# Second attention of an encoder layer: the loads of the values wait for the unit's last exponential, and four transposes and two products get new places

## The chip, the cores and the metric

The kernel runs on one core of one Trainium2 chip. The metric is the device time of one launch in microseconds (us), the median of several runs of the same kernel.

## What is computed

One layer of an encoder, for two groups of 2048 tokens with 1024 features. The change touches the second of its two attentions only:

```
h = rms_norm(x, norm_w);  q_b, k_b, v_b, g_b = parts of h @ w_in
q_b, k_b = rms_norm(q_b), rms_norm(k_b)             # per head, 8 heads of 64
s   = q_b . k_b / 8 + bias(row, col)                # tokens lie on a grid of 32 x 64;
s   = -inf outside the window of 8 rows x 16 cols   # bias is a learned table
o_b = softmax(s) @ v_b * silu(g_b)
x   = x + concat(o_a, o_b) @ w_out;  x = x + (p @ w_ple) * sigmoid(x @ w_ple_gate)
```

## The kernel before

The work runs in three stages: the first attention with its projections (to about 807 us), the second attention (to about 1840 us), and the output products. Every fp32 operand of a large product is split in a high and a low part, and three of the four partial products are summed.

The second attention is done in 64 units (`unit_b(f)`, f from 32 to 95). A unit is 128 queries (8 grid rows x 16 columns) of 4 heads, against 288, 360, 384 or 480 keys, by its place on the grid. Its actions, and the names of their tiles, are:

- `sc(0..3)`, one per head: scores on PE into `scb`; DVE adds the bias and takes the row maximum (`softmax`, L277) into `s`.
- `exp` (`exps`, L301): ACT takes four exponentials. Behind the second, third and fourth of them ACT issues DMAs (L310) that copy the heads' rows `s` into `tn`, a tile of another number type; the last two copies are issued behind the last exponential. In the same action `load_values` issues the loads of the values (L903), three or four DMAs of up to 256 KB on SP's queue, from `v_d` in DRAM into `vw`.
- `fin` of the unit before, `prep` for the next one.
- `pt(0..3)`: PE turns one head's copied rows (`ptb<-rowwise,tn`, L262); ACT and DVE write high and low parts into `p_t`.
- `po(0..3)`: PE multiplies `vw` and `p_t` into `pob`. The first two of these products run at the end of the unit, the last two in the next unit's start.

PE's order is written out and pinned: between the actions a generator hands out the projections of later tiles (24 products `pqk` and 24 `pvg` per unit, 128x512 each), and `PLAN_B` says at which fraction of the unit's budget (10,320 units of cost, 215 for one projection product) each action is put. Its rows are (fraction, 1 for this unit or 0 for the one before, action, index). On the other engines and in SP's queue the compiler layer orders the instructions by the times that it assumes; each queue is then worked through in order.

The bias table of the next unit (L888, `bias`) is loaded with a wait already: `last_ex[0]` is the last exponential issued so far, and `after(load, last_ex[0])` makes a DMA wait for it. The last six units (f of 90 and more) make no copies: their transposes read `s` itself.

SP's queue carries besides: the inputs of later tiles (`stx`, L361), the stores of values (`v_d<-vb`, L846) and results (`ob_d`), and, once in the stage, the new weights for the second half of the heads (`wa<-sp_1wa`, `wb<-sp_1wb`, L197, sixteen loads of 512 KB, issued around 1193 to 1231 us).

Of the kernel before, what the change touches and what calls it, by code (L numbers as in the profile page):

```python
# [11 lines left out]
F32 = mybir.dt.float32  # L12
# [7 lines left out]
NT = SEQ // 128  # L20
# [9 lines left out]
def window(b, cb):  # L30
    c0, nc_ = COL_WIN[cb]
    r0, nr = ROW_WIN[b]
    rows = 5 if nr == 15 and nc_ == 24 else 4
    return r0, nr, c0, nc_, rows


def chunks(nr, rows):

    first = list(range(0, nr - rows, rows)) + [nr - rows]
    return [(k, min(rows, z - k)) for k, z in zip(first, first[1:] + [nr])]  # L40


def row_type(b):
    return (0, 1, 1, 2)[b]


def col_type(cb):
    return (0, 1, 1, 2)[cb]


def query_rows(b, cb, j):

    r0, nr, _, _, rows = window(b, cb)
    k, n = chunks(nr, rows)[j]
    see = [r for r in range(8) if r0 + k - 7 <= min(max(8 * b + r - 4, 0), 24) <= r0 + k + n - 1]
    return (see[0], max(see[-1] + 1, 4)) if see[0] == 0 else (min(see[0], 4), see[-1] + 1)


def bias_offsets():
# [30 lines left out]
AHEAD = 5  # L90
# [8 lines left out]
PLAN_B = (  # L99
    (0.00, 1, "sc", 0), (0.03, 1, "sc", 1), (0.07, 1, "sc", 2), (0.09, 0, "po", 2), (0.11, 1, "sc", 3), (0.16, 0, "po", 3),  # L100
    (0.16, 1, "exp", 0), (0.24, 0, "fin", 0), (0.35, 1, "prep", 0),
    (0.68, 1, "pt", 0), (0.75, 1, "pt", 1), (0.82, 1, "pt", 2), (0.86, 1, "po", 0), (0.90, 1, "pt", 3), (0.95, 1, "po", 1),
)


def emit(ctx, tc, io):
    nc = tc.nc
# [4 lines left out]
    def ptile(shape, tag, name):  # L112
        tag = PSM.get(tag, tag)
        return pp.tile(shape, F32, tag=tag, name=name, bufs=PSB[tag])
# [142 lines left out]
    def mm(out, lhsT, rhs, start, stop):  # L257
        pinned(nc.tensor.matmul(out, lhsT, rhs, start=start, stop=stop))  # L258

    def tr(out, in_, eye=ident):  # L260
        if in_.dtype == F32R:
            pinned(nc.tensor.transpose(out.bitcast(F32R), in_, eye))  # L262
        else:
            pinned(nc.tensor.transpose(out, in_, eye.bitcast(F32)))  # L264
# [8 lines left out]
    def softmax(i, ps, n, bias, sm, s=None):  # L273

        if s is None:
            s = main.tile([128, 512], F32, tag="s", name="s", bufs=SB)[:, :n]
        nc.vector.tensor_tensor_reduce(out=s, in0=ps[:, :n], in1=bias, scale=1.0, scalar=-3.0e38,  # L277
                                       op0=ALU.add, op1=ALU.max, accum_out=sm["mx"][:, i:i + 1])
        sm["s"].append(s)

    def sm_tiles():
        return {"s": [], **{k: ap.tile([128, 4], F32, tag=k, name=k, bufs=3) for k in ("mx", "nm", "den", "rd")}}

    last_ex = []

    def after(ins, other):

        tc.add_manual_dep(ins.ins, other.name, mybir.DependencyInfo(mybir.DependencyClass.Sync, mybir.DependencyReason.DATA),
                          reason="behind the copies")
# [111 lines left out]
    def big(shape, dt, name):  # L401
        return ap.tile(shape, dt, tag="big", name=name, bufs=3)
# [81 lines left out]
    for i in range(2):  # L484
# [5 lines left out]
    v_d = {(half, s, cb): dram.tile([32, COL_WIN[cb][1], 4, 2, HD], F32, tag=f"v_d{half}{s}{cb}", name=f"v_d{half}{s}{cb}")  # L490
           for half in range(2) for s in range(2) for cb in range(4)}
# [382 lines left out]
    def unit_b(f):  # L874
        half, st = divmod(f - 2 * NT, 2 * NT)
        s, j = divmod(st, NT)
        b, cb = divmod(j, 4)
        _, gs = held[f]
        r0, nr, c0, ncol, rows = window(b, cb)
        kc, ch = rows * ncol, chunks(nr, rows)  # L880
        nch, kn = len(ch), [ncol * n for _, n in ch]
        n = nr * ncol
        if cb != 2:
            off, _ = BIAS_OFF[(row_type(b), col_type(cb))]
            if not bt:
                bt.append(big([128, 2, 4, 512], F32, "bias"))
            bt.append(bt[0][:, len(bt) % 2])
            load = nc.sync.dma_start(bt[-1][:, :, :n],  # L888
                                     io["bias"][half][:, off:off + 4 * n].rearrange("p (h n) -> p h n", h=4))
            if last_ex:  # L890
                after(load, last_ex[0])
        bias = bt[-1]
        vw = []

        def load_values():

            spare = f >= 6 * NT - 6 and f % 2 == 0
            if spare:
                four = ap.tile([128, 4, 4, 2 * HD], F32R, tag="raw", name="vw4", bufs=1)
            for j in range(nch):  # L900
                v = four[:, j] if spare else \
                    ap.tile([128, 4, 2 * HD], F32R, tag=("vp", "vr_")[j % 2], name="vw", bufs=3 - j % 2)
                nc.sync.dma_start(v[:kn[j]].bitcast(F32).rearrange("p h d -> p (h d)"),  # L903
                                  v_d[half, s, cb][r0 + ch[j][0]:r0 + sum(ch[j])]
                                  .rearrange("r c h a d -> (r c) (h a d)"))
                vw.append(v)

        sees = [query_rows(b, cb, j) for j in range(nch)]
        order = sorted(range(nch), key=lambda j: sees[j][1] - sees[j][0])
        at = [16 * sum(z - a for a, z in sees[:j]) for j in range(nch + 1)]  # L910
        sm, p_ts, got = sm_tiles(), [], {}

        def sc(h):
            ps = ptile([128, 512], "sc", "scb")
            for j, q in enumerate(qs[f]):
                mm(ps[:, :n].rearrange("p (r c) -> p r c", c=ncol), q[h % 2][:, 128 * (h // 2):128 * (h // 2) + 128],
                   ks_b[h % 2][:, r0:r0 + nr, h // 2, c0:c0 + ncol], j == 0, j == 1)
            softmax(h, ps, n, bias[:, h, :n], sm)
            if h == 3:
                if not tn:  # L920
                    tn.append(ap.tile([128, 4, 480], F32R, tag="ev", name="tn", bufs=1))
                got["ex"] = exps(sm, hr_b[:, st:st + 1], gs, turned=tn[0] if f < 6 * NT - AHEAD - 1 else None)
                next(got["ex"])

        def pt(x):
            h = (0, 2, 1, 3)[x]
            pt = ptile([128, 512], "pt", "ptb")
            for j in order:

                c = at[j] - 16 * sees[j][0]  # L930
                k0 = ncol * ch[j][0]
                tr(pt[:kc, c:c + 128], sm["s"][h][:, k0:k0 + kc], rowwise)
            p_t = main.tile([128, 2, 512], F32R, tag="p_t", name="p_t", bufs=3)
            hi, lo, pf = p_t[:kc, 0, :at[-1]], p_t[:kc, 1, :at[-1]], pt[:kc, :at[-1]]
            nc.scalar.copy(hi, pf)  # L935
            nc.vector.tensor_tensor(out=lo, in0=pf, in1=hi.bitcast(F32), op=ALU.subtract)  # L936
            p_ts.append(p_t)

        def po(x):
            h = (0, 2, 1, 3)[x]  # L940
            e, i = h % 2, h // 2
            if i == 0:
                got["po"] = ptile([128, 2, 256], "ms", "pob")
            if x == 0:
                got["ot"] = ap.tile([128, 2, 2, 128], F32, tag="ot", name="otb", bufs=2)
            po, ot = got["po"], got["ot"]
            for j in order[::-1]:
                a, z = sees[j]
                mm(po[:, i, :].rearrange("p (a q) -> p a q", a=2)[:, :, 16 * a:16 * z], vw[j][:kn[j], h, :],
                   p_ts[x][:kn[j], :, at[j]:at[j + 1]], j == order[-1], j == order[0])  # L950
            if i == 1:
                a, z = 64 * e, 64 - 64 * e
                pq = po.rearrange("p i (a q) -> p i a q", a=2)
                nc.scalar.copy(ot[a:a + 64], pq[z:z + 64])  # L954
                nc.vector.tensor_tensor(out=ot[a:a + 64], in0=pq[a:a + 64], in1=ot[a:a + 64], op=ALU.add)

        def fin(_):
            pgt = ptile([128, 2, 128], "sc", "pgtb")
            for i in range(2):
                tr(pgt[:, i, :], sm["g2"][:, 128 * i:128 * i + 128], rowwise)  # L960
            o_t = ap.tile([128, 2, 128], F32, tag="o_t", name="o_tb", bufs=2)
            nc.gpsimd.tensor_tensor(out=o_t, in0=got["ot"][:, :, 0], in1=got["ot"][:, :, 1], op=ALU.add)
            nc.vector.tensor_tensor(out=o_t, in0=pgt, in1=o_t, op=ALU.mult)
            nc.sync.dma_start(ob_d[s][b, :, 2 * half:2 * half + 2, cb, :], o_t)
        return {"sc": sc, "pt": pt, "po": po, "fin": fin, "prep": lambda _: nxt(f),
                "exp": lambda _: (next(got["ex"]), load_values())}


# [500 lines left out]
```

## Time and profile before

| | us |
|---|---|
| median of 3 runs | 2489.0 (2488.42 to 2490.54) |
| the profiled execution, its own time | 2492.04 |
| its span, first to last instruction | 2490.3 |
| PE busy in the span | 2447.5 (98%) |
| PE weight loads | 2060.5 (83%) |
| DVE, ACT, POOL busy | 1705.6, 1412.8, 853.1 |

The profiled execution is 3.0 us above the median of the runs. PE is busy nearly all the time, so what there is to win or lose from the order of work is in the 43 us in which PE stands still, and in what would be added to them. In a row of the view of waits stand the waiting instruction, what released it, the total of the waits in us, their number, and the longest.

### The profile page before, as it was taken

Reading aid. Unit: us, or ns where it says so; the run is one execution under the profiler, and the core shown is the slowest. Engines: PE = TensorE matmul, PEld = TensorE weight load, DVE = VectorE, ACT = ScalarE, POOL = GpSimd, SP = SyncE. Lnnn points to the kernel's source line nnn. Section 1 sums busy time; section 2 is a strip of 40 time slices with the busy share of each in tenths; the row PEclk is TensorE's granted clock in tenths of the full one; section 3 lists DMA queues with packets and bytes.
Section 4 is the critical chain, followed back from the end, with each engine's and each line's share of the span. In section 5 each row is a group of like instructions: output and inputs, shape, how many; then the busy total and the mean of one; then the engine's idle time right before and its main releaser. Section 6 shows DMA issues by size and latency. Waiting matters only on the chain. (4 is left out here: it accounts for less than half of the span.)

```text
span 2490.3 us, 40934 instructions
## 1 busy us (share of the span) xinstructions
PE 2447.5 (98%) x13062; PEld 2060.5 (83%) x13062; DVE 1705.6 (68%) x4215; ACT 1412.8 (57%) x3408; POOL 853.1 (34%) x1363
## 2 busy tenths in 40 slices
PE   8999999999999999999899999999999999999999
PEld 7888888888888888888778888887777888888887
DVE  6777777777765666666566666776537655686776
ACT  6777777777764665665456566665663222354443
POOL 4555555555543544554344444443110000000000
PEclk9999999999999999999999999999999999999999
DMA  6422233322354677767967787777977455756765
GB/s 208 134 97 94 88 103 98 97 94 87 102 178 153 203 252 234 232 210 228 336 217 228 225 266 255 244 247 266 316 232 272 163 171 175 265 176 217 242 227 170
DMA packets 279288, 485.55 MB, mean 195 GB/s; under 512 B 31617, under 2 KB 120097, under 8 KB 274849
## 3 DMA queue, kind: packets, MB, share of 16 engines
q1 hardware_dynamic: 245376, 437.84, 54.1%
q10 hardware_dynamic: 33696, 45.09, 5.3%
q8 instruction: 104, 1.70, 0.3%
q14 instruction: 112, 0.91, 0.1%
HBM read 307.72 MB, written 134.23 MB: 177 GB/s over the span
## 5 line engine op out<-in xcount | busy, mean ns | idle before, releaser
L258 PE MATMUL pqk<-wa,xr 128*128 128x512 f32 x1536 | 452.5, 411 | 0.0
L258 PE MATMUL pvg<-wb,xr 128*128 128x512 f32 x1536 | 450.6, 406 | 0.0
L301 ACT ACTIVATE s<-s,nm 128x320 f32<-128x320 f32 (+6 forms) x512 | 293.5, 575 | 131.1 <-DVE nm L298 119.1
L258 PEld LDWEIGHTS pvg<-wb,xr 128*128 128x128 f32 x1536 | 272.5, 190 | 34.1
L1254 ACT CAST opd<-raw 128x512 fp32r<-128x512 f32 x224 | 131.7, 619 | 270.6 <-PE acca L1272 117.9
L258 PEld LDWEIGHTS pqk<-wa,xr 128*128 128x128 f32 x1536 | 257.1, 188 | 29.7
L379 POOL TENSOR_TENSOR xr<-stx,xr 128x512 fp32r<-128x512 f32 x186 | 238.6, 1296 | 107.5 <-ACT xr L378 77.7
L1255 DVE TENSOR_TENSOR opd<-raw,opd 128x512 fp32r<-128x512 f32 x224 | 146.6, 686 | 145.6 <-ACT opd L1254 145.6
L258 PE MATMUL pg<-wb,xr 128*128 128x512 f32 x768 | 233.0, 409 | 1.0 <-DVE vv L536 1.0
L258 PE MATMUL pq<-wa,xr 128*128 128x512 f32 x768 | 219.3, 400 | 0.0
L954 ACT COPY otb<-pob 64x512 f32<-64x512 f32 x128 | 74.5, 582 | 213.3 <-PE pob L258 213.1
L936 DVE TENSOR_TENSOR p_t<-ptb,p_t 128x368 fp32r<-128x368 f32 (+5 forms) x256 | 121.6, 487 | 91.3 <-ACT p_t L935 88.7
L1272 PE MATMUL accc<-opd,wb 128*128 128x512 f32 x768 | 177.0, 389 | 0.5 <-DVE r L1317 0.5
L1272 PE MATMUL acca<-opd,wa 128*128 128x512 f32 (+1 forms) x780 | 176.2, 386 | 0.8 <-ACT r L1350 0.5
L1272 PE MATMUL acca<-opd,s 128*128 128x512 f32 x768 | 175.4, 389 | 0.0
L1272 PEld LDWEIGHTS acca<-opd,wa 128*128 128x128 f32 x780 | 144.9, 188 | 30.9 <-ACT ev L1050 0.8
L1272 PEld LDWEIGHTS accc<-opd,wb 128*128 128x128 f32 x768 | 144.1, 188 | 30.8 <-DVE r L1317 1.0
L1272 PEld LDWEIGHTS acca<-opd,s 128*128 128x128 f32 x768 | 144.2, 188 | 29.9
L143 POOL TENSOR_TENSOR yb<-vrb,power 128x8 f32<-128x8 f32 x64 | 106.5, 1664 | 175.7 <-DVE vrb L813 158.0
L935 ACT CAST p_t<-ptb 128x368 fp32r<-128x368 f32 (+5 forms) x256 | 107.5, 427 | 86.5 <-PE ptb L262 74.6
L258 PEld LDWEIGHTS pob<-p_t,vw 128*128 128x128 f32 (+2 forms) x832 | 132.6, 189 | 24.6 <-DVE p_t L936 4.4
L258 PEld LDWEIGHTS pq<-wa,xr 128*128 128x128 f32 x768 | 135.1, 189 | 17.3
(174 smaller groups left out, 5188.1 us busy)
## 6 DMA issues: line engine op xcount, KB each, us to landing
stx<-x_b SPq DMA_DIRECT2D x128, 256.0 KB
vw<-v_d SPq DMA_DIRECT2D x96, 256.0 KB
stx<-x_a SPq DMA_DIRECT2D x64, 256.0 KB
stn<-x_n SPq DMA_DIRECT2D x64, 256.0 KB
v_d<-vb SPq DMA_DIRECT2D x64, 256.0 KB
ple_d<-ev SPq DMA_DIRECT2D x64, 256.0 KB
xres<-x_r SPq DMA_DIRECT2D x64, 256.0 KB
x_d<-r SPq DMA_DIRECT2D x64, 256.0 KB
```

The source lines that it names most:

```text
L143: nc.gpsimd.tensor_tensor(out=y, in0=v, in1=power.broadcast_to([128, n]), op=ALU.pow)
L258: pinned(nc.tensor.matmul(out, lhsT, rhs, start=start, stop=stop))
L301: ex = nc.scalar.activation(ss[i], ss[i], AF.Exp, bias=nm[:, i:i + 1], accum_out=den[:, i:i + 1])
L379: low.tensor_tensor(out=lo, in0=raw, in1=hi.bitcast(F32), op=ALU.subtract)
L935: nc.scalar.copy(hi, pf)
L936: nc.vector.tensor_tensor(out=lo, in0=pf, in1=hi.bitcast(F32), op=ALU.subtract)
L954: nc.scalar.copy(ot[a:a + 64], pq[z:z + 64])
L1254: P(nc.scalar.copy(hi, v))
L1255: P(nc.vector.tensor_tensor(out=lo, in0=v, in1=hi.bitcast(F32), op=ALU.subtract))
L1272: pinned(nc.tensor.matmul(ps[:, cols], w[k][:, a, c:c + 128], o[:, b, cols], start=i in (0, 1, 4) and k == 0 and j == 0, stop=k == 3 and j ...
```

## The change

Two things change. In `PLAN_B` the four transposes `pt` go from 0.68, 0.75, 0.82, 0.90 of the unit to 0.60, 0.68, 0.76, 0.91, and the products `po(0)` and `po(1)` from 0.86 and 0.95 to 0.88 and 0.96. In `load_values` each load of values waits for `last_ex[0]`, which is there the last exponential of the unit that the values are for, in the 58 units that make copies.

```diff
 PLAN_B = (
     (0.00, 1, "sc", 0), (0.03, 1, "sc", 1), (0.07, 1, "sc", 2), (0.09, 0, "po", 2), (0.11, 1, "sc", 3), (0.16, 0, "po", 3),
     (0.16, 1, "exp", 0), (0.24, 0, "fin", 0), (0.35, 1, "prep", 0),
-    (0.68, 1, "pt", 0), (0.75, 1, "pt", 1), (0.82, 1, "pt", 2), (0.86, 1, "po", 0), (0.90, 1, "pt", 3), (0.95, 1, "po", 1),
+    (0.60, 1, "pt", 0), (0.68, 1, "pt", 1), (0.76, 1, "pt", 2), (0.88, 1, "po", 0), (0.91, 1, "pt", 3), (0.96, 1, "po", 1),
 )
...
-                nc.sync.dma_start(v[:kn[j]].bitcast(F32).rearrange("p h d -> p (h d)"),
-                                  v_d[half, s, cb][r0 + ch[j][0]:r0 + sum(ch[j])]
-                                  .rearrange("r c h a d -> (r c) (h a d)"))
+                load = nc.sync.dma_start(v[:kn[j]].bitcast(F32).rearrange("p h d -> p (h d)"),
+                                         v_d[half, s, cb][r0 + ch[j][0]:r0 + sum(ch[j])]
+                                         .rearrange("r c h a d -> (r c) (h a d)"))
+                if f < 6 * NT - AHEAD - 1:
+                    after(load, last_ex[0])
                 vw.append(v)
```

On PE, in the second half of one unit of 384 keys (the rows from the first product of the next tile's `pqk` to the unit's first `po`), before:

```order
L258 MATMUL pqk<-wa_9501,xr 128x512 x3
L258 MATMUL pqk<-wa_9503,xr 128x512 x3
L258 MATMUL pqk<-wa_9505,xr 128x512 x3
L262 MATMUL ptb<-rowwise,tn 128x128 x3
L258 MATMUL pqk<-wa_9507,xr 128x512 x3
L262 MATMUL ptb<-rowwise,tn 128x128 x3
L258 MATMUL pqk<-wa_9509,xr 128x512 x3
L258 MATMUL pqk<-wa_9511,xr 128x512
L262 MATMUL ptb<-rowwise,tn 128x128 x3
L258 MATMUL pqk<-wa_9511,xr 128x512 x2
L258 MATMUL pob<-p_t,vw 128x256
```

and the same place after the change:

```order
L258 MATMUL pqk<-wa_9501,xr 128x512 x3
L258 MATMUL pqk<-wa_9503,xr 128x512 x2
L262 MATMUL ptb<-rowwise,tn 128x128 x3
L258 MATMUL pqk<-wa_9503,xr 128x512
L258 MATMUL pqk<-wa_9505,xr 128x512 x3
L262 MATMUL ptb<-rowwise,tn 128x128 x3
L258 MATMUL pqk<-wa_9507,xr 128x512 x3
L258 MATMUL pqk<-wa_9509,xr 128x512
L262 MATMUL ptb<-rowwise,tn 128x128 x3
L258 MATMUL pqk<-wa_9509,xr 128x512 x2
L258 MATMUL pqk<-wa_9511,xr 128x512 x3
```

The first transposes stand behind 5 projection products instead of 9, the second behind 9 instead of 12, the third behind 13 instead of 16. The first `po` stands behind 19 instead of 18, the last transposes behind 20 as before, the second `po` behind 23 instead of 22.

In SP's queue, from a unit's `ob_d` store of results to the loads of values behind it, in a quiet part of the stage, before:

```order
L964 DMA ob_d_92<-o_tb 128x2x128
L888 DMA bias<-bias 128x4x288
L846 DMA v_d_312<-vb 8x8x512
L846 DMA v_d_313<-vb 16x8x512
L846 DMA v_d_314<-vb 8x8x512
L646 DMA sums_243<-raw 128x2048
L361 DMA stx<-x_b 128x512 x2
L903 DMA vw<-v_d_309 128x512
L903 DMA vw<-v_d_308 96x512
L903 DMA vw<-v_d_309 128x512
```

and another such stretch after:

```order
L966 DMA ob_d_91<-o_tb 128x2x128
L903 DMA vw<-v_d_312 120x512 x3
L888 DMA bias<-bias 128x4x480
L846 DMA v_d_313<-vb 8x8x512
L846 DMA v_d_314<-vb 16x8x512
L846 DMA v_d_315<-vb 8x8x512
L646 DMA sums_243<-raw 128x2048
L361 DMA stx<-x_b 128x512 x2
```

Before, the loads stand ahead of the unit's `ob_d` store, and some of them already fetch values of the next unit; after, all loads of a unit stand behind that store, and the bias table of the next unit stands behind the loads.

Where the new weights come in, SP's queue before (from the second load of `wa` to the inputs `stx`; the numbers at the names count the tensors):

```order
L197 DMA wa_15564<-sp_1wa_211 128x1024
L903 DMA vw<-v_d_308 120x512
L197 DMA wa_15566<-sp_1wa_212 128x1024
L964 DMA ob_d_92<-o_tb 128x2x128
L197 DMA wa_15568<-sp_1wa_213 128x1024
L197 DMA wa_15570<-sp_1wa_214 128x1024
L197 DMA wa_15572<-sp_1wa_215 128x1024
L197 DMA wa_15574<-sp_1wa_216 128x1024
L197 DMA wa_15576<-sp_1wa_217 128x1024
L888 DMA bias<-bias 128x4x480
L846 DMA v_d_309<-vb 8x8x512
```

and after:

```order
L966 DMA ob_d_92<-o_tb 128x2x128
L197 DMA wa_15566<-sp_1wa_212 128x1024
L903 DMA vw<-v_d_308 120x512 x3
L197 DMA wa_15568<-sp_1wa_213 128x1024
L197 DMA wa_15570<-sp_1wa_214 128x1024
L197 DMA wa_15572<-sp_1wa_215 128x1024
L197 DMA wa_15574<-sp_1wa_216 128x1024
L197 DMA wa_15576<-sp_1wa_217 128x1024
L846 DMA v_d_309<-vb 8x8x512
L846 DMA v_d_310<-vb 16x8x512
L846 DMA v_d_311<-vb 8x8x512
L888 DMA bias<-bias 128x4x480
```

Here the third load of `wa` goes behind the `ob_d` store, all three loads of values stand between the third and the fourth `wa`, and the bias table of the next unit goes behind the three stores of values.

## The prediction

> **What bounds the kernel now.** I read the waits of PE first, because PE is busy 98% of the span and a microsecond counts only where PE loses it. The five longest:
>
> ```profile
> PE ptb L262 <- DMA tn<-s: 15.8, 18, 3.1
> PE pk L258 <- issue: 7.3, 1, 7.3
> PE scb L258 <- DVE mx L277: 3.6, 2, 2.5
> PE pple L258 <- DVE qg L850: 1.8, 1, 1.8
> PE pob L258 <- DVE p_t L936: 1.7, 4, 0.8
> ```
>
> The transposes wait 15.8 us in 18 places for the copies `tn`; that is the one wait that the change aims at. A product that waits for the values' landing does not occur among them. Next I cut the second attention into stretches, by busy time, with PE and the DMA share in each (columns: stretch, its length, PE, PEld, DVE, ACT, POOL busy, clock, DMA share, GB/s):
>
> ```profile
> 806.70:1174.60 367.90, 364.59 (x2017) 304.73 (x2016) 244.72 (x620) 221.75 (x528) 181.43 (x205) 1.00 0.72 228
> 1174.60:1285.50 110.90, 100.37 (x536) 80.96 (x535) 64.03 (x162) 58.03 (x139) 45.26 (x53) 0.98 0.88 289
> 1285.50:1683.10 397.60, 395.72 (x2190) 330.56 (x2189) 273.43 (x691) 253.82 (x592) 177.25 (x208) 1.00 0.75 240
> 1683.10:1757.40 74.30, 67.84 (x361) 55.41 (x360) 45.22 (x111) 40.15 (x95) 21.60 (x28) 0.98 0.84 283
> ```
>
> PE stands still for 3.3, 10.5, 1.9 and 6.5 us. The second stretch is the six units in which the new weights are loaded, the fourth the end of the units with copies, where the weights of the output stage come. The waits for `tn` in the same four stretches:
>
> ```profile
> PE ptb L262 <- DMA tn<-s: 2.9, 4, 1.1
> PE ptb L262 <- DMA tn<-s: 9.1, 8, 3.1
> PE ptb L262 <- DMA tn<-s: 1.8, 4, 0.8
> PE ptb L262 <- DMA tn<-s: 1.9, 2, 1.0
> ```
>
> Idle time tells less than the whole in the weights' stretch. The same six kinds of unit stand a second time later, with the same 536 matmuls:
>
> ```profile
> 1174.64:1285.49 110.85, 100.32 (x535) 80.95 (x534) 64.03 (x162) 57.98 (x139) 45.22 (x53) 0.98 0.88 289
> 1444.44:1541.64 97.20, 96.42 (x536) 80.26 (x535) 67.45 (x168) 62.80 (x145) 40.04 (x48) 1.00 0.80 259
> ```
>
> 110.85 - 97.20 = 13.7 us is what the weights' stretch costs.
>
> **Why the copies are late.** One unit of 480 keys, by its timeline on SP, ACT and PE (start, length):
>
> ```profile
> 970.82 1.75 SPq L903 DMA_DIRECT2D vw<-v_d  x4
> 972.54 0.47 ACTq L310 DMA_DIRECT2D tn<-s  x1
> 974.36 0.19 ACT L301 ACTIVATION_READ_ACCUMULATOR s<-s,nm 128x1 f32 x1
> 978.61 0.54 PE L262 MATMUL ptb<-rowwise,tn 128*128 128x128 f32 x4 [1.06 <-DMA tn<-s]
> 981.85 0.57 PE L258 MATMUL pob<-p_t,vw 128*128 128x256 f32 x4
> ```
>
> The four loads of values are issued 1.7 us ahead of the first copy. That copy, 240 KB, lands 6.1 us after its issue (978.61 - 972.54), and PE has stood 1.06 us for it. What the DMA engines moved in three of those microseconds:
>
> ```profile
> 970.40:971.40 1.00, 1.00 (x8) 0.90 (x7) 0.68 (x3) 0.28 (x1) 0.10 (x1) 1.00 0.00 0
> 972.40:973.40 1.00, 1.00 (x7) 0.78 (x6) 0.57 (x3) 1.00 (x5) 0.74 (x1) 1.00 1.00 385
> 973.40:974.40 1.00, 1.00 (x7) 0.84 (x6) 0.30 (x1) 1.00 (x4) 0.00 (x0) 1.00 0.51 96
> ```
>
> Before the loads the engines are idle; then they move 385 KB in a good microsecond and 96 KB in a bad one. The loads (4 x 256 KB) stand ahead of the copies. A second harm is on ACT, which waits with the fourth copy in hand:
>
> ```profile
> ACT q1b L866 <- DMA vw<-v_d: 21.1, 19, 2.9
> ```
>
> **The edits, one by one.** The sum is made against the profiled execution, 2492.04 us, and then moved by the 3.04 us that it lies above the median.
>
> 1. Transposes earlier. A projection product takes 0.24 us at its place; the row for it is in the quiet unit below (9 products from 1023.87 to the transposes at 1026.02: 2.15 / 9). Four places are 1.0 us for the first transposes, three are 0.7 us for the second and third. No work is added: the same matmuls in another order. By itself the edit can only make copies later against PE: at 13 or more of the 18 waits (those at the first transposes) up to 1.0 us each, some 13 us, and more where a copy has been just in time. At its end of the unit, `po(0)` gets 0.24 us more time.
>
> 2. Values' loads later. The copies' issue stays where it is. With nothing ahead, data flow starts about 1.1 us after an issue (loads issued at 1019.56, nothing moved until 1020.60, below), and 240 KB at 385 KB per us take 0.6 us. In the heavy unit the first copy would land at about 974.5 to 975.5. PE without its wait is at the first transposes at 977.55, and 1.0 us earlier after the change, at 976.6. So at least 1 us is spare, and the 6.6 us of waits for copies outside the weights' stretch (2.9 + 1.8 + 1.9) should go. I take 6.0; the bounds are 0 (copies not faster, waits as they are) and 8 (hidden losses beside the waits, as in the weights' stretch). What hid the values' landing till now is the time from 970.82 to 981.85, 11 us. After the change they are issued behind the last exponential, at 974.6 to 976.3 with the same 1.75 us for four issues. Copies 960 KB, store 128 KB and values 1024 KB are 2.1 MB; from 973.6 at 370 KB per us they end at 979.3, with two bad microseconds at 980.8. The first product is at 981.85 - 1.06 + 0.24 = 981.0. That is the tightest place of the change: 0.2 to 1.7 us spare, in 14 units of this size. In a quiet unit there is more:
>
> ```profile
> 1019.56 1.27 SPq L903 DMA_DIRECT2D vw<-v_d  x3
> 1022.36 0.51 ACTq L310 DMA_DIRECT2D tn<-s  x1
> 1022.78 0.19 ACT L301 ACTIVATION_READ_ACCUMULATOR s<-s,nm 128x1 f32 x1
> 1023.87 2.30 PE L258 MATMUL pqk<-wa,xr 128*128 128x512 f32 x9
> 1026.02 0.38 PE L262 MATMUL ptb<-rowwise,tn 128*128 128x128 f32 x3
> 1028.93 0.45 PE L258 MATMUL pob<-p_t,vw 128*128 128x256 f32 x3
> 1019.60:1020.60 1.00, 1.00 (x7) 0.77 (x6) 0.40 (x2) 0.84 (x2) 0.00 (x0) 1.00 0.00 0
> 1024.60:1025.60 1.00, 1.00 (x6) 0.80 (x6) 0.97 (x3) 0.97 (x4) 0.14 (x1) 1.00 0.98 340
> 1026.60:1027.60 1.00, 1.00 (x8) 0.83 (x7) 0.94 (x3) 0.96 (x3) 0.86 (x3) 1.00 0.07 20
> ```
>
> All of its copies and values are through 6 us after the first load's issue, and the engines then idle. The values, issued from 1023.0 on, land at about 1027.2; the product needs them at 1029.2. I charge 1 us for the 14 large units together and nothing for the others; bounds 0 and 14 (1 us each).
>
> 3. SP's queue behind the loads. The bias table now follows them, 1.3 to 1.75 us later than before, and is read by the next unit's first softmax; in the heavy unit the bytes up to its end are the same, so it ends about as late as the idle microseconds at 970 are long, 1 to 2 us. Nearly all of DVE's waits for it (3.3 us in all, three places) are at the weights. Quiet units: nothing. Stores and `stx` behind it have a unit's time to spare; they wait for later results of DVE and POOL, not for SP.
>
> 4. The weights' stretch. SP, DVE, ACT and PE there:
>
> ```profile
> 1199.01 7.13 SPq L197 DMA_DIRECT2D wa<-sp_1wa  x5
> 1203.21 0.47 ACT L866 ACTIVATE q1b<-pqtb,wk 64x256 fp32r<-64x256 f32 x1 [4.09 <-DMA wa<-sp_1wa]
> 1205.24 0.44 PE L262 MATMUL ptb<-rowwise,tn 128*120 128x128 f32 x3 [3.09 <-DMA tn<-s]
> 1206.22 0.38 SPq L888 DMA_DIRECT2D bias<-bias  x1
> 1213.74 1.82 SPq L846 DMA_DIRECT2D v_d<-vb  x3
> 1215.89 0.66 DVE L277 CUSTOM_DVE_ANT_0 s<-scb,bias 128x480 f32<-128x480 f32 x1 [0.93 <-DMA bias<-bias]
> ```
>
> Here 9.1 of the 15.8 us are lost. With one load of `wa` fewer ahead of the copies, and values out of their way in the six units, most of the 13.7 us should go: I put the gain at 9. But the bias table (960 KB) loses its place: it was issued at 1206.22 and now follows three stores that wait for the tile's values, so it goes out where 1213.74 + 1.82 = 1215.6 stands now, and needs 1.1 us and 2.7 us for 960 KB at 350 KB per us: 1219.4 against 1215.89, a softmax 3.5 us later with PE behind it. I charge 4, so the stretch gives 5, with bounds -3 and 11.
>
> 5. The end (1683 to 1757). The same `wa` places fill with the output stage's weights; 2.5 + 1.8 us there are not waits for copies. I charge 0.5 for a bias table 1 us later; bounds -2 and 2.
>
> Sum: 6.0 - 1.0 + 5.0 - 0.5 = 9.5 us. 2492.0 - 9.5 = 2482.5 for an execution like the profiled one, and 2489.0 - 9.5 = 2479.5 for the median.
>
> [...] In the heavy unit the engines moved some 1.2 MB between the first copy's start and its landing, five times its size. [...]
>
> **The rivals.**
>
> - Copies no sooner, transposes earlier (slower). If the loads of values are not what delays the copies (ACT's queue being served beside SP's), each of the 13 waits at first transposes grows by 1.0 us, less some 3 us from emptier queues: about +10, 2499. For it: the copies wait in the weights' stretch too, where `wa` is in the way. Against it: waits outside that stretch fall on the units with four loads. It decides if a first copy still lands later than 4 us after its issue.
> - Values late (slower). If the loads, issued 3.4 to 3.8 us later, land behind the first product, PE waits in every unit for `vw`. At 0.3 us in all 58 units (17 us) the gain is gone and 7 us are lost: 2496. For it: 0.2 us spare in the worst large unit. Against it: 2 us in the quiet one. It decides at 0.16 us per unit (9.5 / 58).
> - The weights' stretch gives nothing: the late bias table and sixteen weight loads in front of the values cost what the copies win. Sum 6.0 - 1.0 + 0 - 0.5 = 4.5: 2484.5, within what can hardly be told. For it: the queue's order. Against it: 9.1 us of waits of one kind there.
>
> **The numbers.** 0.2% of 2489 is 5.0 us, about what a measurement of this kernel can tell from no change. Forecast 0.66, copies no sooner 0.06, values late 0.10, weights' stretch 0.18. The forecast's own range is 2473 to 2483: terms 2 and 4 at their better ends make 8 + 11 - 2.5 = 16.5 us. With the third rival and half of the slower ones the range is 2472.5 to 2489. Faster: the forecast and a part of the third rival, 0.70; same 0.18; slower 0.12.
>
> **What would show it.** Right: waits of PE for `tn` under 4 us in all, ACT's wait for `vw` gone, DMA engines idle until the first copy in each unit; in the weights' stretch a length of 103 to 108 us, with a wait of `scb` for DVE of 3 to 6 us in the unit after the `wa` loads. Wrong: a row `pob <- DMA vw` over 5 us, waits for `tn` still at 10 or more, or a softmax that waits for `bias` in many units.

## The result, and the profile after

The change makes the kernel slower: 2514.99 us median of four runs (2513.53 to 2525.33) against 2488.71 us, a ratio of 1.0115 with a 95% interval of 1.0087 to 1.0143. The prediction was 2479.5 us. The profiled execution is the slowest of the four, its span 2523.5 us, 33.2 us above that of before; what follows accounts for these 33.2 us, of which the median shows 26.

The waits of PE after the change, the five that matter (columns as before: total, times, longest):

```profile
PE pob L258 <- DMA vw<-v_d: 18.6, 33, 2.9
PE scb L258 <- DVE mx L277: 8.4, 2, 6.9
PE ptb L262 <- DMA tn<-s: 7.0, 4, 3.5
PE scb L258 <- DVE p_t L938: 3.2, 1, 3.2
PE pple L258 <- ACT ev L1052: 1.7, 5, 0.7
```

The wait that the change aimed at fell from 15.8 us in 18 places to 7.0 in 4, and ACT's wait for `vw` (21.1 us) is gone. In its place stands a wait that did not exist: the products wait for the values in 33 places. Two waits for DVE follow, one of 6.9 us.

The same stretches as before, each from the same unit to the same unit (stretch, length, busy time of PE, PEld, DVE, ACT, POOL, clock, DMA share, GB/s), with the rest of the kernel as fifth row:

```profile
806.90:1182.30 375.40, 369.19 (x2017) 307.33 (x2016) 240.41 (x620) 221.53 (x528) 181.05 (x205) 1.00 0.68 223
1182.30:1301.70 119.40, 105.22 (x535) 86.06 (x534) 62.99 (x162) 58.44 (x139) 45.04 (x52) 0.93 0.80 265
1301.70:1706.20 404.50, 399.50 (x2190) 331.74 (x2190) 269.42 (x691) 252.37 (x592) 176.77 (x208) 1.00 0.74 238
1706.20:1785.10 78.90, 68.67 (x361) 55.51 (x360) 44.81 (x111) 40.66 (x95) 21.57 (x28) 0.98 0.82 267
1785.10:2523.50 738.40, 726.68 (x3293) 601.64 (x3291) 478.60 (x814) 289.14 (x551) 15.21 (x29) 0.99 0.65 215
```

and the fifth before:

```profile
1757.40:2490.30 732.90, 725.02 (x3293) 598.86 (x3292) 479.18 (x814) 289.63 (x551) 15.24 (x29) 1.00 0.65 216
```

The losses are 7.5, 8.5 (the weights' stretch), 6.9, 4.6 (the end of the units with copies) and 5.5 us. The first and third are the undisturbed units. Taken apart by kind, each unit from its first scores to the next unit's, in us:

| units | before | after |
|---|---|---|
| 13 of 288 keys | 197.4 | 197.5 |
| 14 of 384 keys | 219.9 | 221.2 |
| 10 of 360 keys | 158.6 | 165.4 |
| 6 of 480 keys, no bias table loaded behind their values | 100.9 | 103.8 |
| 6 of 480 keys, a bias table behind | 106.9 | 109.2 |
| weights' stretch, 6 | 110.8 | 119.4 |
| last 3 with copies | 56.1 | 61.6 |

Each column is one execution. Three kernels below leave the ten undisturbed units of 360 keys as they are in the change, and took 162.6, 163.2 and 164.2 us for them, so a row of this table can be off by two or three us; the weights' stretch was 113.9 us in one of them that leaves it, too, as in the change.

**A unit of 480 keys.** Its timeline on ACT, SP and PE (start, length):

```profile
960.61 0.47 ACTq L310 DMA_DIRECT2D tn<-s  x1
962.65 0.47 ACTq L310 DMA_DIRECT2D tn<-s  x1
962.65 2.21 SPq L903 DMA_DIRECT2D vw<-v_d  x4
965.96 1.19 SPq L846 DMA_DIRECT2D v_d<-vb  x2
967.20 0.57 SPq L646 DMA_DIRECT2D sums<-raw  x1
964.53 0.45 PE L262 MATMUL ptb<-rowwise,tn 128*128 128x128 f32 x4
968.87 0.43 PE L258 MATMUL pob<-p_t,vw 128*128 128x256 f32 x2
969.57 0.44 PE L258 MATMUL pob<-p_t,vw 128*128 128x128 f32 x2 [0.27 <-DMA vw<-v_d]
```

and four of its microseconds, with the clock, the DMA engines' share and GB/s (351 GB/s are 351 KB in one microsecond) at the end of each row:

```profile
961.00:962.00 1.00, 1.00 (x7) 0.79 (x6) 0.42 (x1) 1.00 (x5) 0.31 (x1) 1.00 0.26 98
962.00:963.00 1.00, 1.00 (x6) 0.82 (x5) 0.18 (x1) 0.62 (x2) 0.07 (x1) 1.00 0.95 351
964.00:965.00 1.00, 1.00 (x9) 0.82 (x8) 0.97 (x3) 0.44 (x2) 0.39 (x1) 1.00 0.91 203
967.00:968.00 1.00, 1.00 (x9) 0.83 (x8) 0.97 (x3) 0.75 (x3) 0.00 (x0) 1.00 1.07 346
```

The transposes wait for nothing: the copies come in time, as the prediction said. But from the first copy's issue to the first product there are 8.3 us, in which 2.1 MB of copies, store and values must pass; the engines are full from 962 on (a share of 0.91 to 1.07 in each microsecond up to 970), and the values are not all there when the third product needs them, at 969.57. What the engines moved from 961.7, where the first copy starts, to 969.5, in all and on SP's queue (packets, MB, and for the queue the time of its packets as a share of the engines' time):

```profile
DMA packets 1598, 2.59 MB, mean 332 GB/s; under 512 B 163, under 2 KB 931, under 8 KB 1580
q1 hardware_dynamic: 1022, 1.61, 63.3%
```

So 2.59 MB passed, at 332 KB per us. The prediction had 2.1 MB in its sum and 370 KB per us. The other 0.5 MB are on SP's queue: the store and the loads are 1.1 of its 1.61 MB, the rest belongs to what is issued behind the loads, the stores of the next values and the store `sums` (the last two SP rows above). That these bytes go out before the last load has landed is shown; how much sooner it would land without them, no run tells.

**A unit of 360 keys**, SP and PE:

```profile
945.52 1.41 SPq L903 DMA_DIRECT2D vw<-v_d  x3
946.97 0.47 SPq L888 DMA_DIRECT2D bias<-bias  x1
951.75 0.34 PE L258 MATMUL pob<-p_t,vw 120*128 120x256 f32 x1
952.60 0.45 PE L258 MATMUL pob<-p_t,vw 120*128 120x160 f32 x2 [0.52 <-DMA vw<-v_d]
```

PE has the first of its three loads and stands 0.52 us for the next. Behind them, 0.04 us after the last issue, goes the bias table, 960 KB.

**The weights' stretch**, SP, DVE and PE:

```profile
1214.81 0.35 PE L258 MATMUL pob<-p_t,vw 120*128 120x256 f32 x1 [2.87 <-DMA vw<-v_d]
1221.09 1.83 SPq L846 DMA_DIRECT2D v_d<-vb  x3
1222.96 0.46 SPq L888 DMA_DIRECT2D bias<-bias  x1
1230.27 0.66 DVE L277 CUSTOM_DVE_ANT_0 s<-scb,bias 128x480 f32<-128x480 f32 x1 [7.96 <-DMA bias<-bias]
1230.99 0.77 PE L258 MATMUL scb<-ks_b,q1b 128*128 128x480 f32 x1 [6.90 <-DVE mx L277]
```

The bias table does stand behind the three stores, as read from the order; it costs PE 6.9 us, not 4.

**The clock.** Of the 33.2 us, PE's idle time took 17.5, about what the rows of waits above add up to against those of before. Its busy time rose as well, by 15.7 us (2447.5 to 2463.2), for the same matmuls. Four consecutive stretches around a wait of 1.56 us (for `vw`, up to 917.69), and two of the longer stretches at half clock (columns: length, PE busy, clock, DMA share, GB/s):

```profile
911.78:915.20 3.42, 3.42 (x21) 1.00 0.96 341
915.20:918.61 3.41, 1.85 (x13) 0.99 0.92 290
918.61:922.03 3.42, 3.42 (x13) 0.51 0.51 178
922.03:925.44 3.41, 3.41 (x22) 1.00 0.00 0
...
1215.50:1222.30 6.80, 6.48 (x20) 0.50 0.71 280
1819.70:1826.50 6.80, 6.32 (x21) 0.50 0.53 172
```

In the third stretch 13 matmuls run where 21 or 22 fit. Between 900 and 1900 us the clock is at half in 30.6 us after the change, 28.0 of them busy, and in 6.8 us before; half of the difference of busy time, 10.6 us, is lost to it (an estimate: a 128x512 product starts 0.43 us behind the one before it in the third stretch, and 0.23 us in the first). The other 5 us of the rise I did not attribute.

### The profile page after: what moved, and what is told of

Same layout as the page of the kernel before. It is cut to its first block, busy times and chain, and to the rows that moved or that the text cites. A ratio compares the mean times of both kernels' runs of the same rounds, so it can differ in the third digit from the quotient of the medians.

```text
span 2523.5 us, 40869 instructions
## 1 busy us (share of the span) xinstructions
PE 2463.2 (98%) x13062; PEld 2072.5 (82%) x13062; DVE 1694.8 (67%) x4215; ACT 1411.6 (56%) x3408; POOL 851.9 (34%) x1363
## 4 chain that ended last, share of the span: by engine, by line
PE 83%; DMA 9%; ACT 3%; DVE 2%; issue 2%; SPq 1%; POOL 0%; ACTq 0%; DVEq 0%; POOLq 0%
PE acca L1274 14%; PE pvg L258 12%; PE accc L1274 10%; PE pqk L258 9%; DMA vw<-v_d 6%; PE pg L258 6%; PE pq L258 6%; PE scb L258 3%; PE pob L258 3%; PE pk L258 3%; PE po L258 3%; PE sc L258 3%; PE pt L264 2%; PE pple L258 2%; PE ptb L262 1%
## 5 line engine op out<-in xcount | busy, mean ns | idle before, releaser
L258 PEld LDWEIGHTS pqk<-wa,xr 128*128 128x128 f32 x1536 | 266.1, 189 | 35.0
L277 DVE CUSTOM_DVE_ANT_0 s<-scb,bias 128x288 f32<-128x288 f32 (+3 forms) x256 | 136.3, 544 | 51.1 <-PE scb L258 36.4
```

## The experiments

Every kernel was run beside the kernel before on the same chip; the ratios are to those runs (medians of 2490.1 to 2491.6 us there), the times are medians.

| kernel | us | ratio (95%) | PE waits for `tn` | for `vw` |
|---|---|---|---|---|
| before | 2488.7 | | 15.8 | none |
| the change | 2515.0 | 1.0115 (1.0087 to 1.0143) | 7.0 | 18.6 |
| wait alone | 2519.1 | 1.0109 (1.0089 to 1.0129) | 3.2 | 22.3 |
| places alone | 2512.0 | 1.0076 (1.0058 to 1.0093) | 26.8 | none |
| no wait at the weights | 2501.7 | 1.0040 (1.0025 to 1.0054) | 9.8 | 9.5 |
| second exponential | 2496.2 | 1.0023 (1.0014 to 1.0032) | 16.5 | none |
| second exponential, old places | 2488.6 | 0.9991 (0.9983 to 1.0000) | 8.3 | 1.3 |
| split wait, old places | 2481.6 | 0.9964 (0.9950 to 0.9978) | 3.8 | none |
| old places in the last six units | 2511.0 | 1.0078 (1.0064 to 1.0092) | 4.3 | 13.9 |
| one bias table freed | 2507.6 | 1.0070 (1.0056 to 1.0085) | 6.0 | 14.2 |
| split wait, new places | 2479.1 | 0.9949 (0.9937 to 0.9961) | 2.9 | 0.3 |
| split, old places, two tables freed | 2485.2 | 0.9981 (0.9972 to 0.9990) | 17.7 | none |
| wait in quiet units only | 2495.1 | 1.0013 (1.0004 to 1.0022) | 11.1 | 1.4 |
| split wait, mixed places | 2478.2 | 0.9951 (0.9937 to 0.9965) | 5.0 | none |
| a quarter of the bias | 2496.6 | 1.0025 (1.0013 to 1.0036) | 6.2 | 10.6 |

**The change's two halves.** The wait with the old `PLAN_B`:

```diff
-    (0.60, 1, "pt", 0), (0.68, 1, "pt", 1), (0.76, 1, "pt", 2), (0.88, 1, "po", 0), (0.91, 1, "pt", 3), (0.96, 1, "po", 1),
+    (0.68, 1, "pt", 0), (0.75, 1, "pt", 1), (0.82, 1, "pt", 2), (0.86, 1, "po", 0), (0.90, 1, "pt", 3), (0.95, 1, "po", 1),
```

> The places of the transposes and products as before, the wait as in the change. Theory (values late: the loads behind the last exponential land after the first product of the 360- and 480-key units; the new weights' stretch loses to the late bias table; the end loses to the same kind of queue): the first product now stands 0.24 us earlier against the same landing, so 2513 to 2522 us, waits of PE for vw 18 to 25 us, for tn under 7 us. Rival (the earlier transposes and later products are the loss): 2485 to 2492 us.

```profile
PE pob L258 <- DMA vw<-v_d: 22.3, 33, 3.6
PE ptb L262 <- DMA tn<-s: 3.2, 3, 1.6
```

As expected, 2519.1 us and 22.3 us of waits for values: the loss does not need the new places. The other half, the new `PLAN_B` without the wait:

```diff
-                if f < 6 * NT - AHEAD - 1:
-                    after(load, last_ex[0])
```

> The new places, the loads of values without a wait. Theory (values late): no wait for vw at all; the copies land as late as before and the first transposes ask 1.0 us sooner, so waits for tn grow from 15.8 to 25 to 32 us: 2497 to 2506 us, and more if half-clock windows follow. Rival (the places are the loss): 2510 to 2520 us, with the loss elsewhere than in waits for tn.

```profile
PE ptb L262 <- DMA tn<-s: 26.8, 28, 3.0
PE scb L258 <- DVE p_t L936: 5.6, 2, 5.1
PE scb L258 <- DVE mx L277: 4.9, 2, 2.5
```

The waits for copies grew by 11 us as foreseen, but the time is 6 us above my range and inside the rival's, which looked for the loss elsewhere than in these waits. Part of it is elsewhere: the clock is at half for 20.5 us between 900 and 1900 us, against 6.8 before (the mean granted clock of the execution 0.996 against 0.998), and there is the second row. That is a wait that I had not expected. Its longest lies at 1807.6 us, in the last six units: they go by `PLAN_B` too, and there ACT, held for 2.6 and 3.5 us by stores of `ple_d`, has the `p_t` on which the next scores wait behind it. So both halves lose alone, by 21 us and more, and for different reasons. Together they lose no more than one of them; the waits for copies, 26.8 us with the places alone and 7.0 with both, suggest that the wait frees the copies that the places need.

**Where the wait loses.** No wait in the five units of the weights' stretch and the last three with copies:

```diff
-                if f < 6 * NT - AHEAD - 1:
+                if f < 6 * NT - AHEAD - 1 and not 23 <= f - 32 <= 27 and f - 32 < 55:
```

> The change, but without the wait in the five units in which the new weights come (24th to 28th of the stage) and the last three with copies. Theory: the two stretches go back to about 111 and 56 us, losing 8.6 and 5.5 us of the 33 by which the profiled span grew; the late values in the large units stay: 2499 to 2504 us. Rival (these stretches only show a delay from elsewhere, or their loss comes from the places): 2510 to 2516 us.

2501.7 us; the two stretches are 107.1 and 58.5 us long, against 119.4 and 61.6. They are half of the loss or somewhat more. The rest is in the undisturbed large units (162.6 us for the ten of 360 keys) and in the last six. Next, all loads wait for the second exponential (`exps`, then `load_values`):

```diff
+                if n_ == 1:
+                    second_ex[:] = [ex.ins]
...
-                    after(load, last_ex[0])
+                    after(load, second_ex[0])
```

> The change, but the loads of values wait for the second exponential instead of the last: issued 1.3 us sooner. Theory (values late): they land 0.8 to 1.3 us sooner, the 0.3 to 0.7 us that the large units lose is gone, and the bias table is ahead of the stores in the weights' stretch: waits for vw under 6 us, 2 to 4 half-clock windows in place of 9, 2486 to 2496 us. The first copies now share the engines with two loads; if they land over 1 us later the transposes wait again, 2495 to 2505 us. Rival (the places are the loss): 2508 to 2516 us.

```profile
PE ptb L262 <- DMA tn<-s: 16.5, 20, 2.2
```

1.3 us sooner is enough for the values: PE's wait for them does not occur. The copies pay for it, with 16.5 us of waits: 7.4 in the weights' stretch, and in the undisturbed units mostly for the third copy of those of 480 keys (5.2); the time came out at the limit between my two cases, 2496.2 us. In this run the bias table also stands ahead of the stores again, and the weights' stretch takes 107.8 us. The same edit with the old `PLAN_B` (the first diff above):

> Loads of values wait for the second exponential, the places as before the change. Theory (two losses: values late behind the last exponential; and the new places, which ask for the copies 0.7 to 1.0 us sooner and upset the last six units): against the same wait with the new places (2496.2 us) the third copy of the 480-key units, which landed up to 1.2 us after its transposes stood ready, gets 0.7 us, and PE's wait of 2.3 us for p_t in the last units goes with its half-clock window: 2484 to 2491 us, waits for tn 9 to 13 us, none for vw above 3 us. Rival (the places cost nothing once the values are in time): 2494 to 2498 us.

```profile
PE ptb L262 <- DMA tn<-s: 8.3, 13, 1.6
PE pob L258 <- DMA vw<-v_d: 1.3, 3, 0.5
```

2488.6 us: with the transposes later again the waits for copies are half as long, and the time is that of before, neither gain nor loss.

**Bytes ahead.** If the trouble is too many bytes in too short a time, some must go before the copies are issued. The first two loads of each unit (`j` 0 and 1) lose the wait, the others keep the second exponential:

```diff
-                if f < 6 * NT - AHEAD - 1:
-                    after(load, last_ex[0])
+                if f < 6 * NT - AHEAD - 1 and j >= 2:
+                    after(load, second_ex[0])
```

> The places as before the change; the first two loads of values of each unit go as early as before, the third and fourth wait for the second exponential. Theory (in the 480-key units 2.1 MB of copies, store and values come due within 7.5 us, and only bytes moved ahead of the copies' issue take the pressure off): values land with over 1 us spare, two of four loads stand ahead of the first copy there, which lands about 2 us sooner than before: waits for tn 6 to 11 us, 2480 to 2488 us. Rival (it is only the order at the copies that counts, not the bytes ahead): as the run with all loads behind the second exponential.

```profile
PE scb L258 <- DVE mx L277: 7.5, 3, 3.9
PE ptb L262 <- DMA tn<-s: 3.8, 4, 1.8
```

2481.6 us, 0.36% faster than before. In the 49 undisturbed units PE no longer waits for values, and 0.2 us for copies; what is left lies at the weights, those of the second half and those of the output stage. Then the change itself, with nothing altered but the same two loads:

```diff
-                if f < 6 * NT - AHEAD - 1:
+                if f < 6 * NT - AHEAD - 1 and j >= 2:
```

> The change with its places, but the first two loads of values of each unit are free of the wait; the third and fourth wait for the last exponential, as in the change. Theory (the bytes that come due between the copies' issue and the first product are too many, and half the values moved ahead cure that, whatever the wait of the rest): no waits for vw above 3 us in all, the bias table of the 26th unit ahead of the stores again, the losses of the last units stay: 2494 to 2502 us. Rival (it is the last exponential as such that comes too late for any load): vw waits stay above 10 us, 2508 to 2514 us.

```profile
PE scb L258 <- DVE mx L277: 8.0, 3, 3.7
PE ptb L262 <- DMA tn<-s: 2.9, 2, 1.5
PE scb L258 <- DVE p_t L938: 2.0, 1, 2.0
```

2479.1 us, 36 us below the change, and better than I expected by 15: the six heavy 480-key units take 101.2 us against 106.9 before, the weights' stretch 104.1 against 110.8. The wait for the last exponential is harmless, and outside the last six units the new places are too, once half of the values are moved ahead. The third and fourth load are held as long as in the change, and yet PE waits for values 0.3 us instead of 18.6: that is the clearest evidence that the bytes due behind the last exponential are the cause, and not the late issue of these loads by itself.

**The last six units.** The change with the old places there alone (`PLAN_END` is the old `PLAN_B`):

```diff
-            for part, now, act, i in PLAN_A if in_a else PLAN_B:
+            for part, now, act, i in PLAN_A if in_a else PLAN_B if f < 6 * NT - AHEAD - 1 else PLAN_END:
```

> The change, with the old places in the last six units only, which make no copies and whose loads do not wait. Theory (the new places alone cost there 3.2 us of waits of scb for p_t and two half-clock windows, 3.4 us): 2506 to 2511 us, no wait scb on p_t. Rival (that wait only passes on lateness from the weight loads ahead): 2513 to 2517 us.

2511.0 us, at the upper end of what was expected; the interval of its ratio still touches that of the change. PE's wait of `scb` for `p_t` does not occur in it. The same edit on the kernel with the split wait and the new places:

> The kernel in which two loads of values are free and the others wait for the last exponential (2479.1 us), with the old places in the last six units. Theory (the new places cost by themselves in those units): PE's 2.0 us wait of scb for p_t goes, and nothing else: 2474 to 2478 us. Rival (the wait there was only lateness from the weight loads ahead): 2478 to 2481 us.

2478.2 us against 2479.1: not to be told apart. The wait goes with the places: it occurs in six of the seven kernels that have the new places in these units (not in the last of the table) and in none of the eight with the old ones. What it costs in the end is at most a few us.

**The bias tables.** In the change, the tables of three units in the weights' stretch without their wait:

```diff
-            if last_ex:
+            if last_ex and not 25 <= f - 32 <= 27:
```

> The change, but the bias tables of three units of the weights' stretch are loaded without their wait, so that the 26th unit's stands ahead of the stores of values. Theory (the softmax's 8.0 us wait for that table is the stretch's loss): no wait for bias over 2 us there, the stretch falls from 119.4 to 108 to 112 us, the whole to 2504 to 2509 us. Rival (the table is late only because the sixteen weight loads come through the same engines): the stretch stays over 116 us and another wait takes its place, 2511 to 2516 us.

```profile
PE pob L258 <- DMA vw<-v_d: 14.2, 26, 2.9
PE scb L258 <- DVE mx L277: 2.5, 3, 1.5
```

As expected: the 6.9 us wait is gone, the stretch takes 111.4 us, 2507.6 in all. (The kernel with the old places in the last six units, in which the stretch is as in the change, took 113.9 us for it, with a wait of 5.8; of the stretch's 8 us only 2.5 are beyond that spread.) The same idea in the split kernel with the old places failed:

```diff
-            if last_ex:
+            if last_ex and f - 32 not in (25, 57):
```

> The kernel with the split wait and the old places (2481.6 us), with the bias tables of the 26th and the 58th unit loaded without their wait. Theory (what is left there are two softmaxes that wait for these tables, PE 3.9 and 3.0 us behind them): these waits go, with a half-clock window or two: 2473 to 2479 us. Rival (the weight loads take the same microseconds from something else): 2480 to 2483 us.

```profile
PE ptb L262 <- DMA tn<-s: 17.7, 15, 3.6
PE scb L258 <- DVE mx L277: 1.2, 1, 1.2
```

The softmaxes' wait fell from 7.5 to 1.2 us and the copies' rose from 3.8 to 17.7, most of it at the weights (7.4 us in the stretch of the new weights, 8.1 in the last three units with copies): what the softmaxes gained there, the copies lost. 3.6 us slower than without it.

**Is there anything to win in quiet units?** The old places, and in `load_values`:

```diff
-                if f < 6 * NT - AHEAD - 1:
+                if f < 6 * NT - AHEAD - 1 and n in (288, 384):
```

> The old places, and the wait for the last exponential in the units of 288 and 384 keys alone. Theory (these units had copies and values in time before, so there is nothing to win, and with three loads of 256 KB or less nothing to lose): 2487 to 2493 us, no change from before that can be told. Rival (the wait costs in quiet units too): 2496 us and more.

Nothing to win: units of 288 keys took 197.6 us and those of 384 keys 221.9 (before 197.4 and 219.9). The 2495.1 us are 2 above the range; what cost the 0.13% I did not find. In the profiled execution the ten units of 360 keys, which have no wait in this kernel, are longer as well, 161.0 us against 158.6.

**What makes the 360-key units late.** The change with a smaller table:

```diff
-            load = nc.sync.dma_start(bt[-1][:, :, :n],
-                                     io["bias"][half][:, off:off + 4 * n].rearrange("p (h n) -> p h n", h=4))
+            load = nc.sync.dma_start(bt[-1][:, 0:1, :n],
+                                     io["bias"][half][:, off:off + n].rearrange("p (h n) -> p h n", h=1))
...
-            softmax(h, ps, n, bias[:, h, :n], sm)
+            softmax(h, ps, n, bias[:, 0, :n], sm)
```

> The change, with a quarter of each bias table loaded (the first head's, used for all four heads, so the output is another), in the same place of the queue. It tells what makes the values late in the ten undisturbed units of 360 keys, 165.4 us long together against 158.6 before: the next unit's table, issued right behind their loads, or copies, store and values alone. Theory (the table shares the engines with the last two loads): these ten units fall to 158.5 to 161 us, the six 480-key units that no table follows stay at 103 to 105, the whole falls to 2494 to 2505 us. Rival (copies, store and values are too much by themselves): the ten stay above 163.5 us, the whole at 2507 to 2514 us.

```profile
PE pob L258 <- DMA vw<-v_d: 10.6, 31, 1.7
PE scb L258 <- DVE mx L277: 1.8, 2, 1.2
```

The ten units took 162.2 us, between the two cases, and that settles less than it was meant to. The same units, with whole tables behind their loads, took 162.6 us in the kernel with no wait at the weights, 163.2 with one table freed and 164.2 with the old places in the last six units; PE's waits for `vw` in them are 2.9 us here, 3.0 to 3.3 in those three and 4.8 in the change. So the table's bytes cost these units between nothing and 3.2 us, and 3.6 of the 6.8 us are there without them. The whole is 18 us faster than the change, mostly in the weights' stretch (106.7 against 119.4).

## Why the prediction was wrong, step by step

- **Step 2, the copies: right where nothing else is loaded.** The waits for copies in the 49 undisturbed units went from 5.8 to 0.2 us, and ACT's wait for `vw` went. In the last three units with copies they grew, from 0.9 to 5.4 us; why, no run shows.
- **Step 2, the values: the term that failed.** I let 2.1 MB move at 370 KB per us, the rate of a good microsecond, with an allowance for two bad ones, and found 0.2 to 1.7 us spare. In the unit above, 2.59 MB had moved when the last values landed, at 332 KB per us on the average: 0.5 MB of what SP issues behind the loads was not in the sum, and the rate was too high (203 KB in one microsecond, in which the copies meet the first load). At 332 the 2.1 MB alone would have passed by about 968.0, ahead of the first product at 968.87 (an estimate from these numbers); that speaks for the missing bytes more than for the rate, but no run separates the two. (The values themselves are 960 KB there, three loads of 256 and one of 192, not the 1024 of the sum, which changes little.) I charged 1 us for the 480-key units with bounds of 0 and 14. They cost 5.2 us in the twelve undisturbed ones.
- **"Nothing for the others" was wrong.** The quiet unit that I looked at had 384 keys. The 360-key units were never looked at; with a table of 576 to 960 KB behind their loads the ten undisturbed ones cost 6.8 us.
- **Step 3, SP's queue:** I asked when the bias table would land, not what it takes from the loads just ahead of it. The run with a quarter of it does not tell whether it takes anything in the 360-key units (0 to 3.2 us in ten); in the weights' stretch 7 to 13 us went with it (106.7 us against 113.9 and 119.4).
- **Step 4, the weights' stretch:** the right place and the right mechanism, but a table 8.0 us late instead of 3.5, PE 6.9 us behind it, and with 5.7 us of waits for late values on top. A gain of 5 was forecast, a loss of 8.6 measured; with the table freed it is a loss of 0.6. So the table's place explains 2.5 to 8 of these 13.6 us, and the gain of 9 that I put against it did not come either, though the waits for copies there fell from 9.1 to 1.4 us.
- **Step 5, the end:** 0.5 was charged, +5.5 measured for the three units and as much again behind them, part of which belongs to the last six units. Step 1 counted the new places only where the copies are made.
- **Step 1:** the price of the earlier transposes without relief, "some 13 us" of waits for copies, was about right (11); the places alone cost 21 us, as the last six units and the clock come on top.
- **The clock** is in no term: each wait was charged at its own length.
- **The rivals:** "values late" is what happened, with 0.10. Its price of 0.3 us per unit is near the truth for the loads (0.3 to 0.7 in large units, nothing in small ones); I gave it little because of the spare time worked out in step 2, which was the mistake; its 2496 us were still 19 too few, for want of the weights' stretch, the end and the clock. "Copies no sooner" did not happen in the undisturbed units. The third rival put the weights' stretch at no gain, and it was a loss.
- **Copies and loads together:** the DMA records of the 480-key unit above show, from 965.2 to 966.7 us, 122 packets of copies and 144 of loads side by side. So the loads, issued together with the fourth copy at 962.65 us, did not have the engines to themselves there.

## What to carry to other kernels

Moving a transfer out of another's way only helps if the window that it is moved into still holds all bytes that come due there: add up copies, stores, loads and whatever is issued right behind them (here 2.6 MB passed where 2.1 had been counted), and divide by the average rate of a busy stretch (here 332 KB per us), not by that of a good microsecond, for each size of unit. If it does not fit, move half of the bytes ahead instead of all of them back: here that turned 1.15% slower into 0.51% faster. And where a table of places is shared by loops that work differently, look at each of them.

## What the runs showed of the hardware

In the second attention the granted clock fell to half for 3.41 us twice in the profiled execution before the change, and after it three times for 3.41 us and three times for 6.83 us. Within each execution these stretches start whole multiples of 3.413 us apart. I added up PE's idle time in each 3.41 us of that grid in these two executions. Of the stretches at full clock, all four with 2.7 us or more idle were followed by half clock, and none with 1.32 us or less; of the nine between 1.35 and 1.89 us, four were and five were not. The wait of 1.56 us above falls in one of the four: 915.20 to 918.61, with PE busy for 1.85 of the 3.41 us, and 13 matmuls instead of 21 or 22 in the stretch behind it. So it cost some 1.7 us more than its length (an estimate: half of 3.41 us).
